# Two-layer attention encoder: where early weight subtractions run, and which steps keep source order

## Chip, cores and metric

The kernel runs on one core of one Trainium2 chip. The metric is device time in microseconds (us) of the whole program.

## The reference

x is 512 tokens x 1024 channels, float32. Two layers, each `x + mixer(rms_norm(x)) @ w_out`; both mixers have 16 heads of 64.

```python
hn = rms_norm(x, norm_gain[i])
# layer A (mixer_a): 3 dilated window groups (reach 64, 32, 32 with dilation 1, 4, 16)
proj = hn @ w_in                    # 1024 x 10240: q, k, v of three groups, and a gate
q, k = rms_norm(q) , rms_norm(k)    # per head, then windowed attention with T5 bias
o_g, lse_g = dilated_group_attention(q_g, k_g, v_g, bias_g)
y = sum(softmax(lse over g) * o_g) * silu(gate)
x = x + y @ w_out
# layer B (mixer_b): neighbourhood attention on an 8 x 64 grid, bias from b_rpb
proj = hn @ w_in                    # 1024 x 4096: q, k, v, gate
y = softmax(q k^T * scale + bias) v * silu(gate)
x = x + y @ w_out
```

## The kernel before

**Precision.** Every operand of a large matmul is split into two parts of the reduced type fp32r: a cast h and a remainder l = value - h. A product is three matmuls, h*h + h*l + l*h (`mm3`). For a weight block the cast is made on ScalarE (`cast`, tile `wh`) and the subtraction (`rest`, tile `wl`) on VectorE or GpSimd; the turn counter and `pool[0] = [a, b]` send a of every b subtractions to GpSimd.

**Weights.** `Plan` lists the jobs, blocks of 512 or 384 columns, in the order in which they are used. `splits` walks that list: it issues due loads on the SyncE (SP) queue, issues due sums of weight blocks, casts one job, subtracts the job before, and hands out a block when five are ready. The first 16 jobs (`start_jobs`) are for head chunk 0; `mixed` adds jobs for chunks 1 to 7 of layer A.

**Layer A** goes over eight head chunks of 128 channels (`hc`). `main_a(0)` makes plain projections of q and k (`rawq`, `rawk`) with `project_qk`. `main_a(hc)` for the others uses a scheme with seven half-size products in place of eight; four of them take combinations of quarters of normalised x as operands (`mix_h`, `mix_l`, made once in `mix`). It also computes chunk hc - 1's gate and v. Behind these products stand evictions, sums of squares, and `normed`, which makes the per-head norm (`head_norm`, tiles `nv`, `na`, `rs`).

**The side sequence** (`side`) holds the rest: `k_a` and `q_a` transpose and split k and q (`k0h`, `k0l`, `q0h`, `q0l`), `attn_a` makes scores, softmax, the turning of probabilities (`turn`, and `move`: small DMAs from pt to pt), and `weigh`, the product with v. `weighed` multiplies by the gate, and the chunk's output goes to `y_d` in memory; at the end all are read back (`y_back`, tile `yr`) and split by `y_split` into `y_h`, `y_l` for the output projection.

**Order.** TensorE's instructions run in the order in which the program emits them. `run` merges main and side: a counter (`clock[0]`, nanoseconds of estimated matmul time) advances with each matmul, a side step waits for a stamp and a delay on that counter, and `later_on(delay, job)` emits a job when the counter has passed. Where the main sequence yields a key (a guard), the side sequence is emitted at once up to that key, whatever its delays. The guards that matter are `("w", hc - 2)` in the first product of a chunk (weigh of two chunks before), `("scored", hc - 1)` in v0_a, and `("q", hc - 1)` at the first combined product.

Instructions of VectorE, ScalarE, GpSimd and SP are placed by the compiler's list scheduler, which simulates the run and may move them ahead of others; all of them stand on line 85 in the profile, since they go through the helper `Ordered`. While `held[0]` is true, each is pinned to program order. Before the change `held[0]` is true from `hc = 2` on, until the last chunk's k is normed, and within single steps of chunk 0.

**Layer B** then does the same per chunk with `main_b` and `side_b`; its bias tables `gb_d` and `lb_d` are written to memory by `bias_rows` during layer A: load `rp`, negate it, fill `lb`, store both.

Of the kernel before, what the change touches and what calls it, by code (L numbers as in the profile page):

```python
# [4 lines left out]

# [8 lines left out]
F32 = mybir.dt.float32  # L14
# [32 lines left out]
def tile_hybrid_encoder(  # L47
# [24 lines left out]
    held = [False]  # L72

    class Ordered:
# [6 lines left out]
        def __getattr__(self, name):  # L81
            f = getattr(self.engine, name)

            def call(*args, **kw):
                m = f(*args, **kw)  # L85
                return tc.keep_in_program_order(m) if held[0] else m

            return call

    vec, act, pol, syn = (Ordered(e) for e in (nc.vector, nc.scalar, nc.gpsimd, nc.sync))  # L90

# [56 lines left out]
    turn, pool = [0], [[2, 5]]  # L148
# [136 lines left out]
    def splits():  # L285
        casts, queue, due = [], [], plan.loads(lead)
        for at, (raw, c, step, n) in enumerate(plan.jobs):
            pool[0] = [1, 2] if start_jobs <= at < mixed_jobs else [2, 5]
            for r in due.get(at, ()):
                load(r)  # L290
            for add in plan.sums.get(at, ()):
                add()
            casts.append((cast(raw.tile[:, c : c + step], step), n))
            if len(casts) > 1:
                done, m = casts.pop(0)
                queue.append((*rest(*done), m))
            if len(queue) > 4:
                yield queue.pop(0)
        done, m = casts.pop(0)
        queue.append((*rest(*done), m))  # L300
        yield from queue
# [34 lines left out]
    def later_on(delay, job):  # L336

        timers.append((clock[0] + delay, job))
        timers.sort(key=lambda t: t[0])
# [75 lines left out]
    def head_norm(raw, ss, ns, late):  # L415


        rs = wk.tile([P, 32], F32, tag="rs", name="rs")
        rsqrt(vec, rs[:, : 4 * ns], ss[:, : 4 * ns], 4 * ns, 1.0 / DH)

        def scale(i):
            by = rs[:, i * ns : (i + 1) * ns].unsqueeze(2).to_broadcast([P, ns, 64])
            v = raw[:, i, : ns * 64].rearrange("p (a b) -> p a b", b=64)
            return vec.tensor_mul(v, v, by)

        if late:
            later.append(lambda: [tc.keep_in_program_order(scale(i)) for i in range(4)])
            return
        for i in range(4):
            later_on(600 + 600 * i, partial(scale, i)) if held[0] else scale(i)  # L430
# [87 lines left out]
    def mix():  # L518


        x11, x12, x21, x22 = (x_all[:, k : k + KH, t : t + H] for t in (0, H) for k in (0, KH))
        t = wk.tile([P, 2, KH, H], F32, tag="tr", name="mixed", bufs=1)
        a, b = t[:, 0], t[:, 1]

        def put(n, src, eng):
            act.copy(mix_h[:, n], src)
            eng.tensor_sub(mix_l[:, n], src, mix_h[:, n].bitcast(F32))
            stamp["mix", n] = 0

        yield "wait", ("first",), 500  # L530
        yield from first_out()
        yield 1500
        vec.tensor_sub(a, x21, x22)
        put(0, a, pol)
        yield 2000
        vec.tensor_sub(b, a, x11)
        put(1, b, vec)
        yield 2000
        yield from bias_lines()
        yield "wait", ("rawk", 0), 1000  # L540
        vec.tensor_add(b, b, x12)
        put(3, b, pol)
        yield 5000
        vec.tensor_sub(a, x11, x21)
        put(2, a, vec)

    def row_sums(ssq):

# [23 lines left out]
    def bias_rows():  # L572

        rp = wk.tile([P, 248], F32, tag="p", name="rp", bufs=PB)
        tc.keep_in_program_order(syn.dma_start(rp, rpb))

        def fill():
            vec.tensor_scalar(rp, rp, -1.0, None, op0=ALU.mult)
            lb = wk.tile([P, 376], F32, tag="p", name="lb", bufs=PB)
            vec.memset(lb, BIG)  # L580
            vec.tensor_copy(lb[:, 15 * 8 : 31 * 8], rp[:, 7 * 8 : 23 * 8])
            syn.dma_start(gb_d, rp)
            syn.dma_start(lb_d, lb)

        later_on(2500, fill)

    st = {}
    rk = wk.tile([P, 4096], F32, tag="rawk", name="rawk", bufs=1)
# [43 lines left out]
    def normed(raw, ss, ns, key, hc):  # L632

        def go():
            held[0] = held[0] or (hc == 0 and key != "raw")
            head_norm(raw, ss, ns, key == "raw")
            if hc == 0:
                held[0] = False
            st[key, hc] = raw
            stamp[key, hc] = clock[0]  # L640
            if (key, hc) == ("rawk", NHC - 1):
                held[0] = False

        later_on(2200, go) if held[0] else go()

    def first_out():

# [105 lines left out]
    def q_a(hc):  # L753

        yield "wait", ("rawq", hc), (22000, 10500)[hc] if hc < 2 else 8000
        raw = st.pop(("rawq", hc))
        q0h = wk.tile([P, 512], F32R, tag="q0h", name="q0h", bufs=1)
        q0l = wk.tile([P, 512], F32R, tag="q0l", name="q0l", bufs=1)
        k0h = wk.tile([P, EXT], F32R, tag="k0h", name="k0h", bufs=1)
        k0l = wk.tile([P, EXT], F32R, tag="k0l", name="k0l", bufs=1)  # L760
        q12 = wk.tile([P, 2, 512], F32, tag="q12", name="q12", bufs=1)
        tp = bank("tp")
        for i in range(4):
            transpose(tp[:, i * P : i * P + P].rearrange("p (r j) -> p j r", j=4), raw[:, i, 3 * P :])
        act.activation(k0h[:, 64:EXT], tp, AF.Copy, scale=gk[:, 0:1])
        yield 1000
        vec.scalar_tensor_tensor(
            k0l[:, 64:EXT], tp, gk[:, 0:1], k0h[:, 64:EXT].bitcast(F32), op0=ALU.mult, op1=ALU.subtract
        )
        yield 400  # L770
        tp = transpose4(raw, 0)
        act.copy(q0h, tp)
        yield 1000
        vec.tensor_sub(q0l, tp, q0h.bitcast(F32))
        yield 400
        for g in range(2):
            act.copy(q12[:, g, :], transpose4(raw, P + P * g))
            yield
        stamp["q", hc] = 0
        st["q", hc] = q0h, q0l, q12, k0h, k0l  # L780

    def v_a(hc):

        yield "wait", ("vt", hc), 2500
        vt = st.pop(("vt", hc))
        tp = bank("tp")
        for i in range(4):
            transpose(tp[:, i * P : (i + 1) * P], vt[:, i * P : (i + 1) * P])
        st["v0"] = wk.tile([P, 2, 4, P], F32, tag="k12", name="v0", bufs=1)[:, 0]
        act.copy(st["v0"], tp.rearrange("p (i c) -> p i c", i=4))  # L790
        yield
# [66 lines left out]
    def y_split(t, hc):  # L858
        src = t.rearrange("p (t ja x) -> p x ja t", t=4, ja=8)
        h, l = (u[:, hc, :].rearrange("p (x ja t) -> p x ja t", x=16, ja=8) for u in (st["y_h"], st["y_l"]))  # L860
        act.copy(h, src)
        (vec if hc % 2 else pol).tensor_sub(l, src, h.bitcast(F32))
        stamp["ya", hc, "y"] = 0

    def bias_a(hc):
# [30 lines left out]
    class turner:  # L896
# [7 lines left out]
        def put(self, src, n, off):  # L904

            dst = sb(self.t, off, [[32, n // P], [self.run, 4], [1, 32]])
            vec.transpose(dst, src[:, :n].rearrange("p (i b k) -> p i b k", b=4, k=32))
# [21 lines left out]
    def attn_a(hc):  # L929
# [159 lines left out]
        for u in range(2):  # L1089
            for n, tile_ in enumerate(scores(u)):  # L1090
                later_on(400 + 900 * n, partial(least, n, tile_))
            if u:
                stamp["scored", hc] = 0
                for n in range(4):
                    later_on(8000 + 2000 * n, partial(move, n))
            yield 8500
        yield from v_a(hc)
        yield "wait", ("pt", hc), 2500
        st["e", hc + 1] = bias_a(hc + 1)
        if hc == 0:  # L1100
            yield from q_a(hc + 1)
        yield "wait", ("pt", hc), 11500 if hc == 1 else 9000 if hc == NHC - 2 else 7500
        yield "wait", ("gate", hc), 4000
        gt = weighed(hc, (yield from weigh()))
        if hc < NHC - 2:
            send = lambda: tc.keep_in_program_order(syn.dma_start(y_d[:, hc, :], gt))
            later_on(3000, send)
            stamp["w", hc] = 0
            yield
            if hc == 2:  # L1110
                bias_rows()
            if hc:
                yield from q_a(hc + 1)
            return
        back = y_back(range(4), "tr")
# [249 lines left out]

    def main():
        for hc in range(NHC):
            held[0] = hc > 1
            yield from main_a(hc)
        yield from out_product("ya", sink_a)  # L1370
        gap[0] = cycle((500, 500, 800))
        for hc in range(2):
            st["e", hc] = bias_b(hc)
        for hc in range(NHC):
            yield from main_b(hc)
        yield from out_product("yb", sink_b)
# [131 lines left out]
```

## Time and profile before

| | us |
|---|---|
| median of 3 runs | 873.01 (872.75 to 877.14) |
| profiled execution, its own time | 872.77 |
| span of the profile (first to last instruction) | 871.0 |
| TensorE busy | 836.3 |
| VectorE / ScalarE / GpSimd busy | 633.6 / 509.4 / 316.0 |

The times lie on the profiled execution's span: stage hc = 1 of layer A begins near 56 us, its scores for chunk 0 near 86; chunks 3 to 6 take 62 us each; layer A's output projection begins near 530, layer B near 600. In a group row of the profile, "out<-in" names the tiles without buffer numbers, xN the count, then busy time and mean duration; a bracket gives the idle time of the engine before the instruction and what ended it. PE is TensorE's matmul, PEld its weight load, DVE VectorE, ACT ScalarE, POOL GpSimd, SPq the queue of SyncE; PEclk is the clock that TensorE was granted, as a share of full speed.

### The profile page before, as it was taken

To read this page: it belongs to the slowest core of one execution; us is meant where nothing else is said; L and a number is where in the kernel's file an instruction comes from. 1 tells how busy PE (TensorE), PEld (TensorE's weight loads), DVE (VectorE), ACT (ScalarE), POOL (GpSimd) and SP (SyncE) were. 2 spreads that over 40 slices of the span, in tenths; PEclk is the share of its full clock that TensorE was granted. 3 is DMA by queue.
4 is the path that set the end of the run, shared out by engine and by line. 5 is a ranking of instruction groups with operands and counts; after the bars stand their busy time and mean duration, and the time that the engine had idled before them with its cause. 6 is when DMAs were issued, how large, how long until landed. Compare 5 with 4: busy or idle time off the path is not lost.

```text
span 871.0 us, 18142 instructions
## 1 busy us (share of the span) xinstructions
PE 836.3 (96%) x6611; PEld 691.8 (79%) x6611; DVE 633.6 (73%) x1641; ACT 509.4 (58%) x1066; POOL 316.0 (36%) x271
## 2 busy tenths in 40 slices
PE   8978998999998999999999997999999999999997
PEld 6856876877876878878878876889998898889786
DVE  6989993887796777787787777538577667866642
ACT  7655763855764765855946837535466645665440
POOL 5573451452361452452543524012223223332401
PEclk9999999999999999999999998999999999999999
DMA  9344573666776577765775763274264556545212
GB/s 337 131 92 101 153 195 104 136 169 178 133 165 205 121 161 200 146 164 173 158 175 177 146 204 108 84 247 160 82 174 128 149 164 182 157 131 141 82 49 97
DMA packets 56170, 131.98 MB, mean 152 GB/s; under 512 B 7184, under 2 KB 24528, under 8 KB 55952
## 3 DMA queue, kind: packets, MB, share of 16 engines
q1 hardware_dynamic: 49744, 108.78, 40.7%
q0 software_dynamic: 6048, 22.02, 14.7%
q8 instruction: 52, 0.85, 0.4%
q14 instruction: 38, 0.31, 0.1%
q10 hardware_dynamic: 288, 0.01, 0.0%
HBM read 111.73 MB, written 11.72 MB: 142 GB/s over the span
## 4 chain that ended last, share of the span: by engine, by line
PE 72%; DVE 9%; DMA 6%; ACT 6%; issue 4%; POOL 2%; SPq 2%; POOLq 0%; DVEq 0%; ACTq 0%
PE acc L316 60%; PE log L316 5%; PE o L316 4%; PE tp L320 3%; ACT p L85 3%; DMA wraw<-in_w 3%; DVE na L85 2%; SPq L85 2%; DMA rp<-in_rpb 1%; DVE wl L85 1%; DVE rawq L85 1%; DVE rs L85 1%; ACT rawk L85 1%; POOL wl L85 1%; DMA pt<-in_xt 1%
## 5 line engine op out<-in xcount | busy, mean ns | idle before, releaser
L85 POOL TENSOR_TENSOR wl<-wraw,wh 128x512 fp32r<-128x512 f32 (+1 forms) x167 | 221.9, 1335 | 464.7 <-PE acc L316 248.5
L85 ACT CAST wh<-wraw 128x512 fp32r<-128x512 f32 (+1 forms) x360 | 209.8, 593 | 183.0 <-PE acc L316 151.4
L316 PE MATMUL acc<-wh,hn_h 128*128 128x384 f32 (+1 forms) x488 | 187.1, 383 | 7.9 <-ACT rawk L85 4.7
L85 DVE TENSOR_TENSOR wl<-wraw,wh 128x512 fp32r<-128x512 f32 (+1 forms) x193 | 148.3, 770 | 50.0 <-PE acc L316 36.5
L316 PE MATMUL acc<-wl,hn_h 128*128 128x384 f32 (+1 forms) x488 | 177.9, 365 | 1.0 <-DVE wl L85 0.7
L316 PE MATMUL acc<-wh,hn_l 128*128 128x384 f32 (+1 forms) x488 | 178.0, 365 | 0.0
L85 ACT ACTIVATE p<-p,mn 128x256 f32<-128x256 f32 (+2 forms) x248 | 138.0, 585 | 31.9 <-DVE mn L85 31.9
L316 PEld LDWEIGHTS acc<-wh,hn_h 128*128 128x128 f32 x488 | 92.5, 190 | 27.0 <-issue 6.8
L316 PEld LDWEIGHTS acc<-wh,hn_l 128*128 128x128 f32 x488 | 92.4, 189 | 9.9
L316 PEld LDWEIGHTS acc<-wl,hn_h 128*128 128x128 f32 x488 | 92.7, 190 | 9.3 <-DVE wl L85 1.0
L316 PE MATMUL acc<-wh,mix_h 128*128 128x512 f32 x224 | 88.9, 397 | 0.0
L316 PE MATMUL acc<-wl,mix_h 128*128 128x512 f32 x224 | 87.4, 390 | 0.4 <-POOL wl L85 0.4
L316 PE MATMUL acc<-wh,mix_l 128*128 128x512 f32 x224 | 87.5, 390 | 0.0
L316 PE MATMUL acc<-hn_h,wh 128*128 128x512 f32 x192 | 79.0, 411 | 0.3 <-ACT rawb L85 0.2
L316 PE MATMUL acc<-hn_h,wl 128*128 128x512 f32 x192 | 75.3, 392 | 1.4 <-DVE wl L85 1.4
L316 PE MATMUL acc<-hn_l,wh 128*128 128x512 f32 x192 | 75.0, 391 | 0.0
L85 DVE TENSOR_REDUCE ss<-sq 128x4 f32<-128x256 f32 (+1 forms) x96 | 46.4, 502 | 13.9 <-ACT sq L85 7.1
L85 DVE STREAM_TRANSPOSE pt<-p 128x512 f32<-128x512 f32 (+1 forms) x60 | 40.1, 686 | 21.1 <-ACT p L85 21.1
L316 PE MATMUL acc<-y_h,wh 128*128 128x512 f32 x128 | 53.2, 416 | 0.0
L316 PE MATMUL acc<-y_l,wh 128*128 128x512 f32 x128 | 51.0, 399 | 0.0
L316 PE MATMUL acc<-y_h,wl 128*128 128x512 f32 x128 | 50.9, 398 | 0.0
L316 PEld LDWEIGHTS acc<-wh,mix_h 128*128 128x128 f32 x224 | 42.1, 188 | 9.9 <-ACT p L85 1.0
(145 smaller groups left out, 1379.3 us busy)
## 6 DMA issues: line engine op xcount, KB each, us to landing
wraw<-in_w SPq DMA_DIRECT2D x95, 512.0 KB
wraw<-in_w POOLq DMA_DIRECT2D x42, 512.0 KB, 6.9
wraw<-in_w SPq DMA_DIRECT2D x38, 384.0 KB
pt<-pt SPq DMA_DIRECT2D x112, 64.0 KB
td<-tr SPq DMA_DIRECT2D x24, 224.0 KB
pt<-td SPq DMA_DIRECT2D x24, 224.0 KB
e<-l_d SPq DMA_DIRECT2D x32, 112.0 KB
e<-l_d SPq DMA_DIRECT2D x16, 128.0 KB
```

The costliest lines, as they stand in the source:

```text
L85: m = f(*args, **kw)
L316: nc.tensor.matmul(o, l, r, **kw)
L320: nc.tensor.transpose(o, i, ident)
```

## The change

- The first 31 subtractions of weights (all of the first 16 jobs, and 15 of the next) go to VectorE; before, two of five and then one of two went to GpSimd.
- `in_order` pins the instructions inside it to program order. The combinations of x (sum, cast, subtraction) and each `y_split` are put inside it.
- The norm of chunk 0's k is emitted 4000 later on the counter, and the stamp `("rawk", 0)` with it, for which the second pair of combinations waits.
- `held[0]` is true from `hc = 1` on.
- `bias_rows()` of chunk 2 is called before `v_a`, so that `rp` is loaded sooner; its filling is emitted 1500 after weigh.
- A delay of 2500 after `q_a(1)`, and of 1500 before `q_a(hc + 1)` in chunks 1 to 5.

```diff
@@ -87,6 +87,13 @@
 
             return call
 
+    @contextmanager
+    def in_order():
+
+        was, held[0] = held[0], True
+        yield
+        held[0] = was
+
     vec, act, pol, syn = (Ordered(e) for e in (nc.vector, nc.scalar, nc.gpsimd, nc.sync))
 
     def sb(t, off, dims):
@@ -285,7 +292,7 @@
     def splits():
         casts, queue, due = [], [], plan.loads(lead)
         for at, (raw, c, step, n) in enumerate(plan.jobs):
-            pool[0] = [1, 2] if start_jobs <= at < mixed_jobs else [2, 5]
+            pool[0] = [0, 1] if at < start_jobs + 16 else [1, 2] if at < mixed_jobs else [2, 5]
             for r in due.get(at, ()):
                 load(r)
             for add in plan.sums.get(at, ()):
@@ -522,27 +529,25 @@
         t = wk.tile([P, 2, KH, H], F32, tag="tr", name="mixed", bufs=1)
         a, b = t[:, 0], t[:, 1]
 
-        def put(n, src, eng):
-            act.copy(mix_h[:, n], src)
-            eng.tensor_sub(mix_l[:, n], src, mix_h[:, n].bitcast(F32))
+        def put(n, out, op, x, y, eng):
+            with in_order():
+                op(out, x, y)
+                act.copy(mix_h[:, n], out)
+                eng.tensor_sub(mix_l[:, n], out, mix_h[:, n].bitcast(F32))
             stamp["mix", n] = 0
 
         yield "wait", ("first",), 500
         yield from first_out()
         yield 1500
-        vec.tensor_sub(a, x21, x22)
-        put(0, a, pol)
+        put(0, a, vec.tensor_sub, x21, x22, pol)
         yield 2000
-        vec.tensor_sub(b, a, x11)
-        put(1, b, vec)
+        put(1, b, vec.tensor_sub, a, x11, vec)
         yield 2000
         yield from bias_lines()
         yield "wait", ("rawk", 0), 1000
-        vec.tensor_add(b, b, x12)
-        put(3, b, pol)
+        put(3, b, vec.tensor_add, b, x12, pol)
         yield 5000
-        vec.tensor_sub(a, x11, x21)
-        put(2, a, vec)
+        put(2, a, vec.tensor_sub, x11, x21, vec)
 
     def row_sums(ssq):
 
@@ -582,7 +587,7 @@
             syn.dma_start(gb_d, rp)
             syn.dma_start(lb_d, lb)
 
-        later_on(2500, fill)
+        return fill
 
     st = {}
     rk = wk.tile([P, 4096], F32, tag="rawk", name="rawk", bufs=1)
@@ -632,16 +637,19 @@
     def normed(raw, ss, ns, key, hc):
 
         def go():
-            held[0] = held[0] or (hc == 0 and key != "raw")
-            head_norm(raw, ss, ns, key == "raw")
-            if hc == 0:
-                held[0] = False
+            with in_order() if hc == 0 and key != "raw" else nullcontext():
+                head_norm(raw, ss, ns, key == "raw")
             st[key, hc] = raw
             stamp[key, hc] = clock[0]
             if (key, hc) == ("rawk", NHC - 1):
                 held[0] = False
 
-        later_on(2200, go) if held[0] else go()
+        if (key, hc) == ("rawk", 0):
+            later_on(4000, go)
+        elif held[0]:
+            later_on(2200, go)
+        else:
+            go()
 
     def first_out():
 
@@ -858,8 +866,9 @@
     def y_split(t, hc):
         src = t.rearrange("p (t ja x) -> p x ja t", t=4, ja=8)
         h, l = (u[:, hc, :].rearrange("p (x ja t) -> p x ja t", x=16, ja=8) for u in (st["y_h"], st["y_l"]))
-        act.copy(h, src)
-        (vec if hc % 2 else pol).tensor_sub(l, src, h.bitcast(F32))
+        with in_order():
+            act.copy(h, src)
+            (vec if hc % 2 else pol).tensor_sub(l, src, h.bitcast(F32))
         stamp["ya", hc, "y"] = 0
 
     def bias_a(hc):
@@ -1094,11 +1103,13 @@
                 for n in range(4):
                     later_on(8000 + 2000 * n, partial(move, n))
             yield 8500
+        fill = bias_rows() if hc == 2 else None
         yield from v_a(hc)
         yield "wait", ("pt", hc), 2500
         st["e", hc + 1] = bias_a(hc + 1)
         if hc == 0:
             yield from q_a(hc + 1)
+            yield 2500
         yield "wait", ("pt", hc), 11500 if hc == 1 else 9000 if hc == NHC - 2 else 7500
         yield "wait", ("gate", hc), 4000
         gt = weighed(hc, (yield from weigh()))
@@ -1107,9 +1118,10 @@
             later_on(3000, send)
             stamp["w", hc] = 0
             yield
-            if hc == 2:
-                bias_rows()
+            if fill:
+                later_on(1500, fill)
             if hc:
+                yield 1500
                 yield from q_a(hc + 1)
             return
         back = y_back(range(4), "tr")
@@ -1365,7 +1377,7 @@
 
     def main():
         for hc in range(NHC):
-            held[0] = hc > 1
+            held[0] = hc > 0
             yield from main_a(hc)
         yield from out_product("ya", sink_a)
         gap[0] = cycle((500, 500, 800))
```

More of the change, by code (lines that the diff above doesn't have):

```diff
@@ L1 @@
 import math
-from contextlib import ExitStack
+from contextlib import ExitStack, contextmanager, nullcontext
 from functools import partial
```

## The prediction

> **What bounds the kernel now.** I read the page first, then the busy times by stretch, then TensorE's own waits, then the timeline around each of its gaps.
>
> ```profile
> PE 836.3 (96%) x6611; PEld 691.8 (79%) x6611; DVE 633.6 (73%) x1641; ACT 509.4 (58%) x1066; POOL 316.0 (36%) x271
> ```
>
> TensorE (PE) is busy 836.3 of 871.0 us, and the change touches none of its matmuls. It can only win from the 34.7 us in which PE stands still, and from the slow matmuls that follow a pause. So the question is where those lie.
>
> ```profile
> core 0: us, PE busy (x) PEld busy (x) DVE busy (x) ACT busy (x) POOL busy (x), PEclk, DMA share, GB/s
> ...
> 50.00:60.00 10.00, 5.52 (x25) 4.24 (x23) 10.00 (x13) 4.57 (x7) 5.62 (x5) 1.00 0.64 120
> 60.00:70.00 10.00, 8.38 (x28) 6.49 (x29) 9.83 (x11) 4.70 (x10) 7.50 (x6) 0.83 0.48 99
> ...
> 80.00:86.37 6.37, 4.85 (x24) 3.12 (x22) 6.23 (x15) 3.03 (x5) 2.56 (x2) 1.00 0.34 65
> ...
> 130.00:141.00 11.00, 6.94 (x195) 5.79 (x193) 5.54 (x15) 1.51 (x3) 0.56 (x1) 0.84 0.37 98
> ...
> 195.00:206.00 11.00, 9.66 (x158) 7.52 (x157) 10.62 (x28) 5.18 (x10) 2.89 (x3) 1.00 0.95 226
> ...
> 273.00:284.24 11.24, 7.13 (x32) 5.36 (x29) 5.68 (x11) 4.62 (x8) 1.35 (x1) 0.85 0.48 175
> ...
> 346.39:408.51 62.12, 61.93 (x590) 50.05 (x590) 48.70 (x126) 40.65 (x80) 26.40 (x23) 1.00 0.69 169
> ...
> 520.00:540.00 20.00, 14.95 (x75) 11.76 (x72) 14.32 (x25) 15.25 (x23) 8.68 (x7) 0.91 0.41 155
> 540.00:569.00 29.00, 28.99 (x429) 23.64 (x429) 16.46 (x64) 14.28 (x32) 4.00 (x4) 0.94 0.24 74
> ```
>
> Length less PE busy is the idle time; length times (1 - PEclk) is what a lowered clock costs in time. A settled stage (346 to 408) loses 0.19 us, so most of layer A has nothing to give. Four places do:
> - G1, 50 to 70: 4.48 idle, then 0.17 x 10 = 1.7 of clock: 6.2 us.
> - G2, 130 to 141: 4.06 and 0.16 x 11 = 1.8: 5.8 us.
> - G3, 273 to 284: 4.11 and 0.15 x 11.24 = 1.7: 5.8 us.
> - G4, 520 to 569: 5.05 and 0.09 x 20 + 0.06 x 29 = 3.5: 8.6 us.
>
> Three small ones of about 1.5 us each (1.62 in 60:70, 1.52 in 80:86.37, 1.34 in 195:206) have no clock loss of their own. The chain of waits inside the gaps:
>
> ```profile
> PE tp L320 <- DVE k0l L85: 6.7, 2, 4.1
> ...
> PE o L316 <- DVE k0l L85: 2.9, 1, 2.9
> PE log L316 <- ACT k L85: 2.5, 1, 2.5
> ...
> PE tp L320 <- DVE rawk L85: 1.5, 1, 1.5
> ```
>
> No gap is ended by a transfer of weights or by POOL directly; all (G1 below) are ended by a small VectorE (DVE) or ScalarE (ACT) step that came late. That is a matter of order on those engines, which is what the change edits.
>
> **The change, part by part.**
>
> *G1: second pair of x combinations in source order, layer A's first rawk norm 4000 later.*
>
> ```profile
> 56.28 1.21 DVE L85 TENSOR_TENSOR mixed<-mixed,pt 128x1024 f32<-128x1024 f32 x1
> 57.52 1.04 ACT L85 CAST mix_h<-mixed 128x1024 fp32r<-128x1024 f32 x1 [5.27 <-DVE mixed L85]
> 59.51 1.25 ACT L85 ACTIVATE rawk<-acc,rs_n 128x512 f32<-128x512 f32 x2
> 60.24 0.78 PE L316 MATMUL acc<-wh,hn_h 128*128 128x512 f32 x1 [4.72 <-ACT rawk L85]
> ```
>
> In these rows a bracket holds the idle time just before, and who ended it. ACT stood 5.27 us at the cast of a combination whose DVE sum was late; behind it in ACT's queue stood the evictions of rawk, which free the accumulators that PE's next product opens. In the source the combination comes after those evictions; the scheduler had pulled it ahead. Now sum, cast and subtraction of a pair are pinned, and the second pair (3, then 2) waits for the rawk stamp, which comes 4000 later by the emission clock, inside hc = 1, where everything is now pinned. So the casts cannot stand before the evictions. The sums are due for the third and fourth mixed product, five products later, so the delay is covered. G1 goes; I leave 0.2: gain 6.0. What is late next is DVE's work in 60 to 86:
>
> *First 31 subtractions of weights all on DVE.*
>
> ```profile
> L85 DVE TENSOR_TENSOR wl<-wraw,wh x17: 671/691/1798, 6.8 to 86.3; 128x512 fp32r<-128x512 f32 x17
> L85 POOL TENSOR_TENSOR wl<-wraw,wh x15: 1276/1582/3690, 12.2 to 89.9; 128x512 fp32r<-128x512 f32 x15
> ```
> ```profile
> 77.34 3.34 DVE L85 SCALAR_TENSOR_TENSOR rs<-na,rs 128x16 f32<-128x16 f32 x1
> 81.13 0.18 DVE L85 SCALAR_TENSOR_TENSOR rs<-na,rs 128x16 f32<-128x16 f32 x1
> ```
> ```profile
> 77.81 2.82 POOL L85 TENSOR_TENSOR wl<-wraw,wh 128x512 fp32r<-128x512 f32 x2
> ```
> ```profile
> L85 DVE SCALAR_TENSOR_TENSOR rs<-na,rs 128x32 f32<-128x32 f32 (+1 forms) x6 | 6.4, 1075 | 0.2
> L85 DVE SCALAR_TENSOR_TENSOR na<-na,nv 128x4 f32<-128x4 f32 (+2 forms) x9 | 5.8, 647 | 0.2
> ```
>
> POOL had the 15 rows (min/median/max ns); by the turn counter 14 of them move (the last, at 89.9, stays). They add 14 x 0.69 = 9.7 us to an engine that is full: 10.00, 9.83 and 6.23 in the stretches above. But the same step on DVE takes 0.18 us alone and 3.34 us while two subtractions run on POOL, so that pair held DVE 3.16 us, and on DVE it costs 1.38. In 20 to 86 the last two groups alone lose 6.4 - 6 x 0.18 = 5.3 and 5.8 - 9 x 0.18 = 4.2 us in this way, a part of it to other POOL work. Bounds for DVE's time: +9.7 if no subtraction had held it, 14 x (0.69 - 1.58) = -12.5 if each had like that pair. I take zero, near the middle and near the sum of the two groups (9.5 against 9.7). On PE's path the pair at 77.81 ended in the 1.5 us wait for rawk; that goes, and half of the wait in 60:70: gain 2.
>
> *G2: hc = 1 in source order.*
>
> ```profile
> 131.67 1.43 DVE L85 TENSOR_TENSOR rawk<-rawk,rs 128x256 f32<-128x256 f32 x4
> 133.62 0.75 DVE L85 SCALAR_TENSOR_TENSOR k0l<-tp,gk,k0h 128x512 fp32r<-128x512 f32 x1
> ```
> ```profile
> 134.42 0.43 PE L316 MATMUL o<-pt,rawk 32*64 32x128 f32 x4 [2.95 <-DVE k0l L85]
> ```
>
> ```profile
> 129.23 1.03 PE L320 MATMUL tp<-ident,rawq 128*128 128x128 f32 x8
> ```
>
> At 129 the main sequence reaches its guard on weigh(0) and forces q_a(1) and weigh(0) out at once. The four output banks of weigh must be read out first, and DVE had the whole rawk norm ahead of k0l and q0l. In source order that norm comes out 2200 later and its four scalings 600 apart, so k0l and most of q0l go ahead of the scalings, but not ahead of the eleven small steps before them. On the other side rawq's stamp is also 2200 later, so q_a(1) starts later against the same guard, and the 2500 added behind it does nothing, since the forced pass ignores delays. I take 2 us of the 4.06 as left and half the clock loss: gain 5.8 - 2.9 = 2.9. Bounds: the gap stays whole (0) or goes (5.8). The Trainium skill (TensorE: Matmul & The Clock Gate, What's actually happening) lets the clock fall after an idle window of about 3.4 us. By that a rest of 2 us costs no clock and the gain would be 3.8. The trace does not side with it: in G4 two pauses of 2.6 and 2.5 us were enough, while 1.34 and 1.5 us were not.
>
> *1500 before q_a in hc 1 to 5.* In 195:206 PE waited 1.34 us at the first transpose of q_a, because the output banks had not been read; the delay fills that with matmuls: gain 1.3. In the settled stages there is no such wait; scores come 1.5 us later, but the second half of them is fixed by the guard in v0_a, and 0.19 us per stage says that nothing else is tight there: zero.
>
> *G3: rp loaded before weigh(2), its filling after.*
>
> ```profile
> 254.51 10.09 SPq L85 DMA_DIRECT2D e<-l_d  x6
> ...
> 266.55 0.42 SPq L85 DMA_DIRECT2D rp<-in_rpb  x1
> ```
> ```profile
> 277.18 0.29 DVE L85 TENSOR_SCALAR rp<-rp 128x248 f32<-128x248 f32 x1 [7.43 <-DMA rp<-in_rpb]
> ...
> 278.04 0.75 DVE L85 SCALAR_TENSOR_TENSOR k0l<-tp,gk,k0h 128x512 fp32r<-128x512 f32 x1
> ```
>
> ```profile
> 237.45 0.60 PE L320 MATMUL tp<-ident,vt 128*128 128x128 f32 x4
> ```
>
> SP took 10 us over six loads of bias rows, so rp went out at 266.55 and landed 10.6 us later; DVE, pinned, stood 7.43 us at the negation of rp, with k0l behind it. Now rp is issued ahead of v_a(2), whose transposes stand at 237.45, ahead of those six loads, 25 us before its use. It can wait there for a buffer of tag p, with the moves of pt behind it, but the turns that free it are done by then. The filling (under 1 us of DVE) still stands before k0l and no longer waits. Late next would be the weights; PE holds some four casts in hand. Gain 5.6 of 5.8.
>
> *G4: y_split in order.*
>
> ```profile
> 524.23 4.16 ACT L85 CAST y_h<-yr 128x512 fp32r<-128x512 f32 x4 [2.84 <-DMA yr<-y_d]
> 528.81 0.68 ACT L85 ACTIVATE k0h<-tp,gk 128x512 fp32r<-128x512 f32 x1
> ...
> 537.34 2.02 ACT L85 CAST y_h<-yr 128x512 fp32r<-128x512 f32 x2 [0.95 <-DMA yr<-y_d]
> ```
>
> All four returned outputs were cast in a row, and k0h behind them was 4.16 us late; the same later with two casts before the second k. In order, two casts (2.1 us) remain before k0h and the others come with their timers, 7 and 9 us on. That halves the first wait and takes most of the second, but the wait for yr itself stays, and q_a(7) is not pinned, so the scheduler is free to do otherwise. Bounds 0 and 8.6; I take 3.0.
>
> *New waits.* Pinning hc = 1 puts casts of weights behind each cast that waits for DVE, and q_a(0), k_a(0) and the scores of hc 0 move some 4 us along the main sequence. The nearest rows for one such misfit are the small waits of 1.34 to 1.5; I charge two: 2.9.
>
> Sum: 6.0 + 2 + 2.9 + 1.3 + 5.6 + 3.0 - 2.9 = 17.9. The profiled execution took 872.77 us (span 871.0 and 1.8 around it), in line with the median of 873.01. 872.8 - 17.9 = 854.9, told as 855.
>
> **The rivals.**
>
> *All gaps close.* G1 to G4 and the small ones are 26.4 + 4.5 = 30.9, so 842 is the floor; 846 with two misfits. For it: all are order. Against: the load of yr and the forced pass at G2 do not change.
>
> *Only the load of rp works.* The order of DVE at 55 to 86 and 130 stays as late as it is: 872.8 - 5.6 = 867. Against: G1 has its cause in plain sight.
>
> *A new gap at weigh(0).* The scores of hc 0 go out some 4.5 us later and with them the 16 moves of pt, on an SP that is now in order too.
>
> ```profile
> 121.61 5.69 SPq L85 DMA_DIRECT2D pt<-pt  x8
> ```
> ```profile
> 139.04 2.09 PE L316 MATMUL o<-pt,v 128*64 128x64 f32 x64
> ```
>
> The last moves were issued by 127.3, and the half that needs them begins at 139.0. Of these 11.7 us the later scores take 4.5 and the shorter gap 2; about 5 are left, less the landing. If SP is held up by 10 us more, PE waits some 8 with the clock loss of 1.8, and nothing is gained at G2: 854.9 + 2.9 + 9.8 = 868, and with a second misfit of that kind among the loads of weights up to 877; 872 for the middle. For: the moves follow the scores by fixed delays. Against: the slack.
>
> *Slower: VectorE becomes the bound from 10 to 86.* If POOL's subtractions held DVE for less than 0.69 us each, the 9.7 us are added to an engine without slack, G1 only changes its cause, and each of two new pauses costs 1.75 of clock: 872.8 + 9.7 + 3.5 - 5.6 = 880. The decisive point is that 0.69. For: DVE is at 98% there. Against: 3.34 against 0.18. The Trainium skill (Perfetto Trace Analysis, Optimizing Scalar/DVE Operations) speaks for this rival where it says that a saturated DVE may be relieved by moving work to GpSimd, and against it where it adds that the two share a read port; the 3.34 us row sides with the second half.
>
> **How the numbers follow.** Forecast, within 850 to 862: 0.55. All gaps close, 842 to 850: 0.13. Less than forecast, down to the 867 of rp alone: 0.14. New gap at weigh(0), or as much lost elsewhere, 869 to 877: 0.09. VectorE the bound, 877 and over: 0.09. About 0.5% (4.4 us; the three runs spread that far) is what a measurement can tell from no change; faster by more means under 868.6: 0.55 + 0.13 + 0.14 = 0.82. Same 0.09, slower 0.09. The range of 845 to 870 leaves out the last two cases and a little of the second.
>
> **What would show it.** Right: PE idle down from 34.7 to about 22 us; no wait of PE for rawk near 56; rp issued some 25 us before its negation, which waits for nothing; no POOL subtraction of weights before about 85; stretched small steps of DVE between 60 and 86 gone; one shorter pause at weigh(0). Wrong: a wait of PE for wl in the first 90 us (VectorE the bound), for pt at the moved half of weigh(0), or for wh behind a waiting cast in hc = 1; G4 as long as before.

## The result, and the profile after

The changed kernel takes 864.25 us (median of 4 runs, 861.94 to 865.57); the kernel before, run beside it, 874.48 (872.75 to 877.14). The ratio is 0.9878, 95% interval 0.9838 to 0.9917: faster by 1.2%, where 855 us had been forecast with a range of 845 to 870. The profiled execution took 865.5 (span 863.7) against 872.77 (871.0): the two traces explain 7.3 us of the 10.2 between the medians. A few single executions in these runs took over 150 us longer; all medians here are of the others.

The page's line of engines, of the changed kernel:

```profile
PE 838.7 (97%) x6611; PEld 693.6 (80%) x6611; DVE 630.8 (73%) x1655; ACT 509.1 (59%) x1066; POOL 288.7 (33%) x257
```

PE stands still for 863.7 - 838.7 = 25.0 us, down from 34.7. To place the difference I compared when PE ends the same work in both traces:

| PE has ended | before | after | this stretch |
|---|---|---|---|
| weigh(0) | 141.13 | 141.71 | +0.6 |
| mixed products of chunk 3 | 251.04 | 250.08 | -1.5 |
| mixed products of chunk 4 | 319.08 | 313.48 | -4.6 |
| weigh(7) | 569.08 | 561.90 | -1.6 |
| all | 871.0 | 863.7 | -0.1 |

The table says at once where the forecast went wrong. The stretches with the delay before q_a (to chunk 3), with rp (to chunk 4) and with the returned outputs (to weigh(7)) changed by 1.5, 4.6 and 1.6, where 1.3, 5.6 and 3.0 had been forecast. The first 141 us, where 8 us were to be won (6.0 at G1, 2 small waits, 2.9 at weigh(0), less 2.9), are 0.6 longer than before. Within them the changed kernel was ahead for a while: PE ends chunk 1's mixed products at 109.42, where it had been 112.58, and loses these 3.2 us again before weigh(0) is done.

Busy times by stretch, of the changed kernel (length, then each engine's busy time, PEclk, share and rate of the transfers):

```profile
core 0: us, PE busy (x) PEld busy (x) DVE busy (x) ACT busy (x) POOL busy (x), PEclk, DMA share, GB/s
50.00:95.00 45.00, 39.91 (x243) 31.66 (x242) 38.09 (x66) 27.25 (x51) 17.44 (x13) 0.96 0.54 123
115.00:145.00 30.00, 25.00 (x269) 20.06 (x268) 22.26 (x50) 12.43 (x23) 8.37 (x7) 0.83 0.55 132
...
20.00:86.30 66.30, 61.69 (x281) 49.17 (x280) 58.11 (x106) 37.71 (x68) 15.71 (x11) 0.97 0.41 110
255.00:285.00 30.00, 29.29 (x318) 23.56 (x317) 23.29 (x60) 14.99 (x29) 9.81 (x8) 1.00 0.69 187
```

The same stretches of the kernel before:

```profile
50.00:95.00 45.00, 36.84 (x226) 28.41 (x225) 42.78 (x81) 26.89 (x53) 22.75 (x17) 0.96 0.49 107
115.00:145.00 30.00, 25.72 (x285) 21.21 (x284) 21.37 (x49) 11.84 (x22) 8.45 (x7) 0.94 0.58 153
...
20.00:86.30 66.30, 58.14 (x259) 45.09 (x257) 61.52 (x92) 36.82 (x64) 38.77 (x25) 0.97 0.44 112
255.00:285.00 30.00, 25.89 (x239) 20.71 (x237) 20.55 (x48) 12.84 (x23) 7.63 (x7) 0.94 0.72 189
```

Idle time and clock loss as in the prediction: from 50 to 95 they were 8.2 + 1.8 and are 5.1 + 1.8, so 3.1 won. From 115 to 145 they were 4.3 + 1.8 and are 5.0 + 5.1, so 4.0 lost. What the first stretch wins, the second pays back. Who ends the pauses, by PE's waits of the changed kernel (total, times, longest):

```profile
PE acc L323 <- DVE wl L85: 7.3, 4, 3.1
...
PE o L323 <- DVE k0l L85: 1.8, 1, 1.8
...
PE tp L327 <- DVE k0l L85: 1.2, 1, 1.2
```

The waits for a late k0l, 6.7 + 2.9 us before, are 1.8 + 1.2. In their place stand waits for `wl`, the subtracted part of a weight block; the kernel before had 2.1 us of them, 1.38 in one place from 50 to 145. The timeline of PE shows them:

```profile
65.21 0.50 PE L323 MATMUL acc<-hn_h,wl 128*128 128x512 f32 x1 [3.07 <-DVE wl L85]
82.52 0.50 PE L323 MATMUL acc<-wl,mix_h 128*128 128x512 f32 x1 [1.52 <-DVE wl L85]
...
123.80 0.80 PE L323 MATMUL acc<-wl,hn_h 128*128 128x512 f32 x1 [2.34 <-DVE wl L85]
134.24 0.69 PE L323 MATMUL o<-pt,rawk 32*64 32x128 f32 x4 [1.83 <-DVE k0l L85]
279.60 0.38 PE L323 MATMUL log<-k0h,q0h 64*128 64x256 f32 x1 [0.71 <-ACT k L85]
```

And the timeline of DVE shows why `wl` was late:

```profile
61.97 0.42 DVE L85 TENSOR_REDUCE ss<-sq 128x4 f32<-128x256 f32 x1 [1.25 <-ACT sq L85]
63.31 0.42 DVE L85 TENSOR_REDUCE ss<-sq 128x4 f32<-128x256 f32 x1 [0.92 <-ACT sq L85]
64.14 0.42 DVE L85 TENSOR_REDUCE ss<-sq 128x4 f32<-128x256 f32 x1 [0.41 <-ACT sq L85]
64.48 1.88 DVE L85 TENSOR_TENSOR wl<-wraw,wh 128x512 fp32r<-128x512 f32 x3
...
120.64 2.50 DVE L85 TENSOR_TENSOR rawq<-rawq,rs 128x512 f32<-128x512 f32 x4
123.06 1.29 DVE L85 TENSOR_TENSOR wl<-wraw,wh 128x512 fp32r<-128x512 f32 x2
```

Around 62 DVE is not full; it stands idle, 1.25 + 0.92 + 0.41 us, before three sums of squares that wait for ScalarE, with three subtractions of weights pinned behind them. At 120 it scales rawq for 2.50 us, with the subtraction that PE waits for behind it. Both look like the price of source order in chunk 1; the experiment with chunk 1 not pinned tests it.

### The profile page after: what moved, and what is told of

Its sections match the earlier page's. It is cut to its first block, busy times and chain, and to the rows that moved or that the text cites. A ratio compares the mean times of both kernels' runs of the same rounds, so it can differ in the third digit from the quotient of the medians.

```text
span 863.7 us, 18127 instructions
## 1 busy us (share of the span) xinstructions
PE 838.7 (97%) x6611; PEld 693.6 (80%) x6611; DVE 630.8 (73%) x1655; ACT 509.1 (59%) x1066; POOL 288.7 (33%) x257
## 5 line engine op out<-in xcount | busy, mean ns | idle before, releaser
L85 POOL TENSOR_TENSOR wl<-wraw,wh 128x512 fp32r<-128x512 f32 (+1 forms) x153 | 197.8, 1294 | 448.5 <-PE acc L323 227.8
L85 DVE TENSOR_TENSOR wl<-wraw,wh 128x512 fp32r<-128x512 f32 (+1 forms) x207 | 160.4, 779 | 49.3 <-PE acc L323 34.5
L323 PEld LDWEIGHTS acc<-wl,mix_h 128*128 128x128 f32 x224 | 42.1, 188 | 11.0 <-DVE wl L85 2.0
```

The costliest lines, as they stand in the source:

```text
L323: nc.tensor.matmul(o, l, r, **kw)
```

## The experiments

Each was run beside the kernel before on the same chip; ratios are to that; the changed kernel itself was run again beside three of them.

**The changed kernel again.** No edit.

> The changed kernel itself, unaltered, timed beside the three that follow so that they can be set against it: 862 to 866, ratio to the kernel before 0.986 to 0.990.

864.34 us, 0.9894 (0.9877 to 0.9911). This is what the experiments that start from the changed kernel are compared with, best by the ratios, since three of them (chunk 1 not pinned, GpSimd's share as before, y_split without order) ran on another chip. Its 50 to 95 and 115 to 145 are idle and slowed as in the first profile (39.90 and 24.99 busy, PEclk 0.96 and 0.83), so the new waits belong to the program.

**The load of rp alone**, in the kernel before:

```
+        fill = bias_rows() if hc == 2 else None
         yield from v_a(hc)
...
-            if hc == 2:
-                bias_rows()
+            if fill:
+                later_on(1500, fill)
```

> The kernel before with one part of the change: rp loaded ahead of v_a of chunk 2, its filling 1500 after weigh. Theory (the stall at 273 to 284 was VectorE standing at rp): VectorE waits 0 for rp, PE's 4.1 us there fall to under 1, nothing else moves; 5 to 6 us faster than before, 867 to 869. Rival (the weights are what is late there: ScalarE waits 3.5 us for wraw in the same place): PE waits for wh or wl instead, gain under 2 us.

870.26 us against 874.36, 0.9951 (0.9932 to 0.9969): 4.1 us, where 5 to 6 had been expected. In its row of the stretch the pause shrinks:

```profile
255.00:285.00 30.00, 28.14 (x309) 22.63 (x308) 22.23 (x57) 12.52 (x23) 8.27 (x7) 0.96 0.70 189
```

Idle 1.86 for 4.11. What is left is a wait for k that ScalarE evicts late; in the changed kernel that rest is 0.71 at the same place. The cause of G3 is shown: one 0.5 us issue in the wrong place on SP cost four microseconds.

**Chunk 1 not pinned**, in the changed kernel:

```
-            held[0] = hc > 0
+            held[0] = hc > 1
```

> The changed kernel with everything pinned from chunk 2 on only, as before. Theory (source order in chunk 1 makes the new waits for wl at 62 and 121, 3.07 and 2.34 us with 1.7 us of clock each): both go, and some of the old wait at weigh(0) comes back; 2 to 6 us faster than the changed kernel, about 860. Rival (VectorE has too much work there after taking 14 subtractions over): both waits stay within 1 us, time within 2 us of the changed kernel.

860.78 us, 0.9844 (0.9816 to 0.9873), the fastest median of all. Its interval lies just below that of the changed kernel run again (0.9873 against 0.9877), the only one that does, and overlaps that of the changed kernel's first runs. PE's timeline from 50 to 145:

```profile
79.59 0.57 PE L327 MATMUL tp<-ident,rawk 128*128 128x128 f32 x2 [3.23 <-DVE rawk L85]
81.31 0.81 PE L327 MATMUL tp<-ident,rawk 128*128 128x128 f32 x2 [1.14 <-DVE rawk L85]
120.54 0.30 PE L327 MATMUL tp<-ident,rawq 128*128 128x128 f32 x1 [1.32 <-DVE rawq L85]
132.31 0.69 PE L323 MATMUL o<-pt,rawk 32*64 32x128 f32 x4 [1.69 <-DVE k0l L85]
```

No wait for `wl` is left in this stretch, and no wait for the evictions of rawk comes back. So the source order of chunk 1 made the waits for `wl`, and G1 stays closed without it. The free scheduler has waits of its own, at 79 to 81, as long as the one at 65 was; weigh(0) ends at 139.97, 1.4 us sooner than in the changed kernel run again (141.39), and the mixed products of chunk 4 at 311.16 against 313.54. By the ratios the gain is some 4 us, of which these profiles explain a part: from 50 to 145 idle time and clock loss together fall only from 17.0 to 15.8 us, and where the rest comes from is not shown.

**GpSimd's share as before**, in the changed kernel:

```
-            pool[0] = [0, 1] if at < start_jobs + 16 else [1, 2] if at < mixed_jobs else [2, 5]
+            pool[0] = [1, 2] if start_jobs <= at < mixed_jobs else [2, 5]
```

> The changed kernel with the first 31 subtractions shared with GpSimd as before. Theory (source order makes the new waits): the waits for wl at 62 and 121 stay, small VectorE steps stretch again while GpSimd subtracts; 0 to 5 us slower than the changed kernel. Rival (VectorE is overloaded by the 14 subtractions, 9.7 us of work): the waits at 62 and 82 shrink by 3 us or more, 3 to 6 us faster than the changed kernel.

865.69 us, 0.9897 (0.9863 to 0.9931): no difference from the changed kernel. PE's waits in its timeline:

```profile
57.65 0.50 PE L323 MATMUL acc<-wh,hn_h 128*128 128x512 f32 x1 [1.93 <-ACT rawk L85]
65.05 0.50 PE L323 MATMUL acc<-hn_h,wl 128*128 128x512 f32 x1 [1.18 <-DVE wl L85]
83.70 0.66 PE L327 MATMUL tp<-ident,rawk 128*128 128x128 f32 x4 [1.91 <-DVE k0l L85]
125.06 0.64 PE L323 MATMUL acc<-wl,hn_h 128*128 128x512 f32 x1 [2.33 <-DVE wl L85]
```

The wait at 65 fell by 1.9, but 1.93 for rawk's evictions came back just ahead of it, which gave DVE as much time; the one at 124 did not move. With chunk 1 pinned, where the subtractions run moves the pauses and wins nothing. ScalarE's timeline shows that the wait for rawk has its old cause, a cast that waits for a late combination, although the pairs are pinned here:

```profile
55.44 1.04 ACT L85 CAST mix_h<-mixed 128x1024 fp32r<-128x1024 f32 x1 [2.01 <-DVE mixed L85]
...
56.91 1.83 ACT L85 ACTIVATE rawk<-acc,rs_n 128x512 f32<-128x512 f32 x3
```

**The sharing alone**: the first 31 subtractions on VectorE and nothing else, in the kernel before (`[0, 1] if at < start_jobs + 16`).

> The kernel before with one part of the change: the first 31 subtractions all on VectorE. Theory (a subtraction on GpSimd holds VectorE about as long as the subtraction takes there): VectorE's busy time in 20 to 86 stays within 3 us, the stretched small steps at 63 and 77 go, the old wait for rawk at 56 stays; within 2 us of the kernel before. Rival (VectorE is overloaded by 9.7 us more): new waits for wl in the first 90 us, 4 to 8 us slower.

876.83 us against 873.91, 1.0033 (1.0019 to 1.0047): 2.9 us slower. DVE is not the bound: from 20 to 86.3 it is busy 57.64 us, less than the 61.52 before. The wait for rawk near 56 is gone, with no pair pinned: ScalarE waits 0.91 us at the cast of 56.57, where it waited 5.27, and two evictions of rawk stand ahead of it. Two other waits are there, in PE's timeline:

```profile
66.81 2.19 PE L320 MATMUL tp<-ident,rawq 128*128 128x128 f32 x4 [4.06 <-DVE rawq L85]
82.10 1.24 PE L320 MATMUL tp<-ident,rawk 128*128 128x128 f32 x4 [2.73 <-DVE rawk L85]
```

Neither account was right: no overload, only one new wait for `wl` (1.06 us at 19.48), and the old wait did not stay; but there is no gain either. From 50 to 95 PE's idle time falls from 8.2 to 7.1 us, and PEclk from 0.96 to 0.89, which is 3 us more of clock in the profiled execution.

**y_split without order**, in the changed kernel (the `with in_order()` of y_split taken out).

> The changed kernel with y_split left to the scheduler as before. Theory (order of the casts of returned outputs makes the pauses at 520 to 540): four casts in a row ahead of k0h again, PE's pauses there back from 3.6 to about 5 us with more clock loss; 1.5 to 4 us slower than the changed kernel. Rival (the load of yr sets both pauses): the pauses stay near 3.6 us, time within 1 us.

867.47 us, 0.9931 (0.9902 to 0.996): about 3 us slower than the changed kernel, with an interval that overlaps its own a little. G4's two waits are back in PE's timeline:

```profile
526.88 1.11 PE L327 MATMUL tp<-ident,rawk 128*128 128x128 f32 x4 [4.26 <-DVE k0l L85]
535.21 0.38 PE L323 MATMUL log<-k0h,q0h 64*128 64x256 f32 x1 [1.20 <-ACT k L85]
```

In the changed kernel they are 1.16 at 524.46 and none at 535; two new ones, 1.86 at 528.92 and 0.57 at 530.46, wait for other evictions of ScalarE. ScalarE's timeline of the changed kernel shows what the prediction had described, two casts of returned outputs ahead of k0h in place of four:

```profile
520.13 2.10 ACT L85 CAST y_h<-yr 128x512 fp32r<-128x512 f32 x2 [3.86 <-DMA yr<-y_d]
...
522.66 0.69 ACT L85 ACTIVATE k0h<-tp,gk 128x512 fp32r<-128x512 f32 x1
```

Without the order the four casts stand in a row ahead of k0h again, for 4.12 us from 519.64. From the end of weigh(6) to that of weigh(7) PE takes 53.15 us in the kernel before and 53.08 here, 51.59 in the changed kernel's first profile and 49.07 in its second.

**Without the delays of 2500 and 1500**, in the changed kernel (both lines taken out).

> The changed kernel without the delays of 1500 and 2500 around q_a. Theory (the 1500 fills the wait for the output banks of weigh in chunk 2 and costs nothing elsewhere, the 2500 does nothing): PE waits 1.3 us again near 203, nothing else; 1 to 2 us slower than the changed kernel. Rival (the later q_a costs in the settled stages): the settled stages shrink, time the same or up to 2 us faster.

865.27 us, 0.9898 (0.9881 to 0.9915): 0.9 us slower by the medians, which the intervals do not resolve. The place is as expected, though: PE stands 1.69 us at 204.79, at q_a's first transpose, where the changed kernel has no pause.

**Without the 4000 before chunk 0's norm of k**, in the changed kernel:

```
-        if (key, hc) == ("rawk", 0):
-            later_on(4000, go)
-        elif held[0]:
+        if held[0]:
```

> The changed kernel without the 4000 for chunk 0's k norm: it goes at once, and the second pair of combinations 4 us earlier. Theory (the delay is what takes the second pair's casts from in front of the evictions of rawk): PE waits 3 to 5 us for rawk near 56 again with 1.7 of clock; 3 to 6 us slower than the changed kernel. Rival (pinning the pairs is enough, since in source order they stand behind the evictions): no wait for rawk over 1 us, time within 2 us of the changed kernel.

862.08 us, 0.9857 (0.9837 to 0.9878). No wait for rawk near 56: the delay that was to close G1 is not what closes it, and the loss of 3 to 6 us that the theory expected is not there; by the ratios the kernel is some 3 us faster than the changed one, with intervals that touch. The pauses in PE's timeline change their sizes:

```profile
65.73 0.50 PE L323 MATMUL acc<-hn_h,wl 128*128 128x512 f32 x1 [4.11 <-DVE wl L85]
...
131.72 0.69 PE L323 MATMUL o<-pt,rawk 32*64 32x128 f32 x4 [3.44 <-DVE k0l L85]
```

**Four ways to keep the gains and lose the new waits.** The first emits the three squares of chunk 0's k, on which DVE stood at 62, 800 later:

```
+            if (key, hc) == ("rawk", 0):
+                later_on(800, partial(squares, raw[:, i, : ns * 64], ss, i, ns, True))
+                return
```

> The changed kernel, where only the squares and row sums of chunk 0's k are emitted 800 and 1600 later, so that two of the four sums no longer stand ahead of the first subtractions of chunk 1 on VectorE. Theory (the wait for wl at 62, 3.07 us, is the queue behind sums that wait for ScalarE's squares): that wait falls to 1 to 2 us and its clock loss of 1.7 us goes, the wait at 121 stays; 2 to 4 us faster than the changed kernel. Rival (VectorE is simply full there): the wait moves a few us on and the time stays within 1 us.

862.73 us, 0.9864 (0.9842 to 0.9886), less gain than the theory's 2 to 4 us. The wait at 65 falls from 3.07 to 0.90; those at 76 and 81 come to 1.15 and 2.32, so of 2.2 us won 2.0 is given back as idle time. The 1.6 us by medians are not resolved; in the profiles the rest is clock: from 50 to 145 PEclk is 0.95 for 0.93, 1.9 us in 95. The second also ends the pinning once chunk 1's rawq is normed:

```
         if hc == 1:
+            held[0] = False
             yield from v0_a(hc - 1)
```

> As the kernel with squares later, and pinning is lifted from the last product with a combination in chunk 1 to the end of that chunk. Theory (source order makes both waits for wl): the wait at 121 (2.34 us and 1.7 of clock) goes as it did with pinning from chunk 2 on, and the start of chunk 1 keeps its order; 4 to 8 us faster than the changed kernel, 856 to 860, the fastest so far. Rival (work on VectorE at 110 to 135 is too much in any order): a wait of 2 to 4 us at the forced weigh of chunk 0 takes its place, time as with squares later.

861.11 us, 0.9856 (0.983 to 0.9882). The `wl` wait at 124 goes, leaving 1.34 for rawq, and weigh(0)'s grows from 1.83 to 3.12 (at 132.97), as the rival had it.

The third leaves chunk 1 unpinned and takes the 4000 out:

> The changed kernel with pinning from chunk 2 on only, and without the 4000 for chunk 0's k norm. Theory (with chunk 1 free, the only large new wait was for the normed k of chunk 0, 3.23 and 1.14 us, because its norm was emitted late): that wait falls under 1.5 us, no old wait for rawk near 56 over 1 us; 2 to 5 us faster than the changed kernel with pinning from chunk 2, 856 to 859. Rival (the small steps of that norm are put behind the subtractions of weights whenever chunk 1 is free): the wait stays within 1 us, time about 861.

863.17 us, 0.9882 (0.9863 to 0.99). The wait for the norm of k at 76 to 81 does not go; it is 5.00 us at 76.35, and the time is not below that with chunk 1 not pinned. The fourth takes the 4000 out and ends the pinning early:

> The changed kernel without the 4000, and with pinning lifted from the last product with a combination in chunk 1 to that chunk's end. Theory (source order at both ends of chunk 1 makes the waits): the wait for wl at 121 goes, the one at 62 to 66 (4.1 us without the 4000) stays; 1 to 3 us faster than the changed kernel, about 861. Rival: the forced weigh of chunk 0 takes over what is won, as it did with squares later and release (3.12 us there); time as the changed kernel without the 4000, 862.

862.58 us, 0.9868 (0.9851 to 0.9885). The wait at 66 stays at 4.12, that at 124 goes, and the one at weigh(0) is 4.06. The rival held here. None of the four beats chunk 1 not pinned alone, and what each cures in one place comes back in the next: the four cures don't add.

## Why the prediction was right or wrong

The time came out inside the range and on the side that was forecast, but not in the band of 850 to 862: it lies in the case "less than forecast", which had a chance of 0.14. The gains at G3 and G4 came nearly as reckoned. The first 141 us were reckoned wrongly, and the total is in the range because that reached down to the gain of rp alone.

**G1, the old wait: gone, but not for the reason I gave; its term of 6.0 was too much.** My step was that sum and cast, pinned, cannot stand before the evictions of rawk. It holds for the second pair, but it is not what closed the wait. The wait of PE for rawk near 56 is there in every run that shares the early subtractions with GpSimd (4.72 before, 4.61 with rp alone, 1.93 with GpSimd's share as before), and in no run that has them on DVE, the sharing alone included, which pins no pair. So the moved subtractions close it, which I had credited with other waits; order without them left 1.93. The change did take the second pair away: its casts were at 50.16 and 57.52 and are at 72.84 and 79.22, where ScalarE now waits 7.25 and 3.08 us for them. But the first pair, pinned too, came in its place. Its casts were at 40.91 and 43.72 and are at 52.42 and 58.08, the latter still ahead of two evictions of rawk, in ScalarE's timeline of the changed kernel, with a wait of 2.40 us. The 4000 that I named as the cover is not needed. No run took the pinning of the pairs out by itself, so what it is worth stays open.

```profile
58.08 1.06 ACT L85 CAST mix_h<-mixed 128x1024 fp32r<-128x1024 f32 x1 [2.40 <-DVE mixed L85]
59.04 0.68 ACT L85 ACTIVATE rawk<-acc,rs_n 128x512 f32<-128x512 f32 x1
```

In the sum, what failed is "G1 goes; I leave 0.2". I had named DVE's work from 60 to 86 as late next and given it no price, because the chain I followed ended at the cast. The next in line stood in the trace of before, in PE's timeline:

```profile
69.42 0.51 PE L316 MATMUL acc<-hn_h,wl 128*128 128x512 f32 x1 [1.38 <-DVE wl L85]
```

It is the product that now starts at 65.21. PE comes to it 5.9 us sooner, and its `wl`, now behind the sums of squares, only 4.2: the 4.72 won at 56 gives 1.7 back here, 3.07 for 1.38, with the clock at 0.83 (last section) as after the old wait.

**The 31 subtractions: near in what DVE pays, wrong in what PE gains.** The stretched small steps are gone. Two groups of DVE from 20 to 86.3 (busy, mean ns), in the changed kernel and then with GpSimd's share as before:

```profile
L85 DVE SCALAR_TENSOR_TENSOR na<-na,nv 128x4 f32<-128x4 f32 (+2 forms) x9 | 1.6, 175 | 0.2
...
L85 DVE SCALAR_TENSOR_TENSOR rs<-na,rs 128x32 f32<-128x32 f32 (+1 forms) x6 | 1.1, 180 | 0.2
```
```profile
L85 DVE SCALAR_TENSOR_TENSOR na<-na,nv 128x4 f32<-128x4 f32 (+2 forms) x9 | 2.7, 297 | 0.2
L85 DVE SCALAR_TENSOR_TENSOR rs<-na,rs 128x32 f32<-128x32 f32 (+1 forms) x6 | 2.1, 352 | 0.2
```

The two groups fell from 5.8 and 6.4 us to 1.6 and 1.1, as much as the 9.5 that the prediction read as held time. But 7.4 of it is gone without the move too (GpSimd's share as before), and with the move alone a third group (na<-rs) grew from 2.1 to 5.3 as these two fell: which steps are stretched changes with the order as well. I had taken zero for what the move adds to DVE's busy time in this stretch: it adds 3.0 us with chunk 1 pinned (58.11 against 55.15) and takes 3.9 off in the kernel before (57.64 against 61.52). What PE gains is the old wait for rawk, and that much came back elsewhere: giving GpSimd its share back costs nothing, and the sharing alone loses 2.9 us. The gain of 2 was taken from two waits as if nothing came next. The rival in which VectorE becomes the bound is refuted: it is busy 58.11 of 66.30 us.

**G2 and the new waits: the mis-sized term.** I charged 2.9 us for "two misfits" of 1.34 to 1.5 us without clock loss. Waits for `wl` went from 2.1 to 7.3 us, 3.07, 1.52 and 2.34 in the stretches in question. The stretch of 115 to 145, for which the sum had a gain of 2.9 at weigh(0) and at most the two misfits, loses 4.0 us: the wait at weigh(0) did fall, from 2.95 and 0.77 to 1.83 and 0.24, but 2.34 came ahead of it and the clock loss rose by 3.3. "Wrong: a wait of PE for wl in the first 90 us" is what happened, with another cause than the one I attached to it: order, not load. The profile had a sign of it: in chunk 1 DVE had little slack (busy 42.78 of 45.00 us from 50 to 95 before), and a pinned step that waits holds up all that stand behind it, as at 62. Taken over the first 145 us, PE's idle time fell by about 3.4 us and the clock loss rose by 3.3, in place of the 8.0 that the sum had there.

**G3, 5.6: right in place, 4.1 alone and 4.6 here** from 251 us to the end of chunk 4's mixed products. The rows of the tile rp, in the changed kernel (shortest, median and longest in ns; first and last start):

```profile
L85 SPq DMA_DIRECT2D rp<-in_rpb x1: 518/518/518, 243.4 to 243.4; - x1
L85 DVE TENSOR_SCALAR rp<-rp x1: 284/284/284, 268.3 to 268.3; 128x248 f32<-128x248 f32 x1
```

It is loaded 25 us ahead of its negation, as forecast, and nothing waits for it. The rest is a wait for k behind a cast on ScalarE, and that cast waits for a load of weights: what I had named as late next.

**G4, 3.0: about right.** Taking the order out costs about 3 us. The first profile of the changed kernel shows a gain of only 1.6 up to weigh(7), because it lost 3.3 us of clock there that the second did not (below); the second shows 4.1 from weigh(6) to weigh(7). **1500 before q_a, 1.3:** the pause returns without it, 1.69 us; the total shows 0.9, unresolved.

Summed as the prediction did: 4.6 (rp), about 3 (y_split) and about 1 (unresolved) came; of the 8.0 net in the first 141 us nothing came. 17.9 - 8.0 = 9.9, against 10.2 between the medians and 7.3 in the profiled pair, which holds those 3.3 us of clock. One sum of the prediction is off without effect: the floor of 842 with two misfits of 2.9 is 845, not 846.

What stays open is whether an order exists that closes both 50 to 95 and 115 to 145. The lowest median of those run, chunk 1 unpinned, is 860.78 us, and most of the others cannot be told from it.

## What to carry to other kernels

Pinning an engine to source order removes waits that a scheduler made by pulling a step ahead, and makes new ones wherever the source puts a step with a late input ahead of urgent work; here the stage in which VectorE had little slack was faster unpinned. When several edits act on one pause, run each alone before naming the one that closed it: here the pause at G1 went with the edit that had been credited with others. When a wait is removed, price the second-latest input of the same consumer before booking the gain: here the 8 us forecast went to waits for `wl` just behind and to the clock after them, and one of these waits stood in the profile of before as 1.38 us. A load that stands behind a row of issues on one queue was cheap to move here, and its gain came within 1.5 us of the forecast.

## What the runs showed of the hardware

**The clock does not follow the length of a pause alone.** In the changed kernel the pause of 3.07 us at 62 leaves 0.83, that of 2.34 at 121 as much, and the 1.83 us at 132 leaves 0.72, in its stretches:

```profile
60.00:70.00 10.00, 6.93 (x24) 5.28 (x23) 7.04 (x22) 5.59 (x13) 2.11 (x2) 0.83 0.47 105
...
120.00:130.00 10.00, 7.66 (x31) 5.89 (x30) 9.69 (x20) 3.78 (x7) 4.58 (x5) 0.83 0.65 133
130.00:142.00 12.00, 9.58 (x205) 8.02 (x204) 5.86 (x16) 2.08 (x4) 1.08 (x1) 0.72 0.55 140
...
530.00:540.00 10.00, 9.54 (x96) 7.39 (x97) 5.04 (x24) 8.27 (x18) 2.79 (x2) 0.67 0.15 55
```

The 0.67 follows pauses of 1.16, 1.86 and 0.57 us. The same program run again has 1.28, 1.89 and 0.56 there and pays nothing:

```profile
530.00:540.00 10.00, 9.04 (x105) 6.70 (x107) 6.70 (x27) 9.99 (x21) 2.87 (x2) 1.00 0.26 88
```

That is 0.33 x 10 = 3.3 us between two executions of one kernel. The Trainium skill (TensorE: Matmul & The Clock Gate, What's actually happening) puts the fall after an idle window of about 3.4 us and calls the window free-running, so that runs vary. The variation agrees with these two rows; that a pause must be 3.4 us long does not, since none in these rows was. In slices of 1 us the first profile of the changed kernel has 0.50 from 66 to 69, 124 to 127, 134 to 140 and 530 to 536, and 1.00 soon before and after: each loss is half of about 3.4 us or of twice that. I had priced a pause's clock at 1.75 us each; the rows show 0, 1.7 and 3.4 (0.28 x 12 from 130 to 142).

**A step can be held longer than any one step that it overlaps.** A GpSimd subtraction of 128x512 took 1.28 us at 60.61 in the changed kernel, where DVE stood idle beside most of it. With the sharing alone one took 7.30 us beside a row of DVE steps without a gap, and a DVE step that takes 0.19 at 64.82 took 4.44 beside two GpSimd subtractions in a row, of 2.69 and 1.54 us; both stand in that kernel's timelines of GpSimd and DVE, and spans on GpSimd are rough:

```profile
52.31 7.30 POOL L85 TENSOR_TENSOR hn_l<-pt,hn_h 128x512 fp32r<-128x512 f32 x1 [1.64 <-ACT hn_h L85]
60.17 2.69 POOL L85 TENSOR_TENSOR mix_l<-mixed,mix_h 128x1024 fp32r<-128x1024 f32 x1
```
```profile
59.69 4.44 DVE L85 TENSOR_TENSOR na<-rs 128x32 f32<-128x32 f32 x1
```

That kernel has no weight subtraction on GpSimd before 91 us; the ones that overlap here are of the normalised x and of its combinations. So moving the weight subtractions did not end the long steps. I take this as part of why that edit alone won nothing; no run separated it.
